# Seven block products instead of eight in the feed-forwards of a two-layer trunk

## The chip, the cores and the metric

The kernel runs on one core of a Trainium2 chip. The metric is device time in microseconds (us). The kernel before took 2554.37 us, the median of three runs (2552.99 to 2556.95). The engines are named as the profile names them: PE is TensorE's matmul side, PEld its weight loads, DVE is VectorE, ACT is ScalarE, POOL is GpSimd, SP is SyncE, whose queue issues the loads of weights.

## The reference, cut to what matters

Two layers act on 128 prompt tokens and 512 sample tokens (640 together, T), with 1024 features. Each layer has a gated feed-forward, a mixer, and a second feed-forward; the mixer of layer 0 is a convolution beside a recurrent scan, that of layer 1 is windowed attention. All is float32.

```python
def swiglu(h, w_in, w_out):
    gt, up = jnp.split(h @ w_in, 2, axis=-1)
    return (jax.nn.silu(gt) * up) @ w_out

def ffn_sublayer(x, mod, g, w_in, w_out, slot):
    h = pre_norm(x, g, mod[:, 3 * slot], mod[:, 3 * slot + 1])
    return x + 0.5 * mod[:, 3 * slot + 2] * swiglu(h, w_in, w_out)
```

`w_in` is 1024 x 5632 (2816 gate and 2816 value features), `w_out` is 2816 x 1024. `mod` is the modulation: `silu(cond) @ w_mod[l] + b_mod[l]`, nine slots of 1024 features per layer, for the two conditions (prompt and sample). There are four feed-forwards; below they are called FFN 1 to 4 (layer 0 first, layer 0 second, layer 1 first, layer 1 second).

## The kernel before, in words

Activations lie feature-major: a tile is 128 features by 640 tokens. A float32 product is made exact by splitting each operand into a high and a low part (`split_x`, L515: a cast on ACT gives the high part, a subtraction on DVE the low part) and summing three products on PE: high*high, high*low, low*high (`product_steps`, L523).

A feed-forward (`ffn`, L554) runs in parts of 8, 8 and 6 tiles of 128 hidden features (`PARTS`). For each hidden tile it loads a 1024 x 128 slice of the gate's weights (`raw_wg`) and one of the value's (`raw_wu`), splits both, and for two chunks of tokens (`CHUNKS`: 256 and 384 columns) sums 8 blocks x 3 terms into a PSUM bank for the gate (`pg`) and one for the value (`pu`). ACT applies silu to `pg`, DVE multiplies by `pu`, and the result `g` is split again. After a part, `project_out` (L591) sums the part's hidden tiles through `w_out` into `po`, and DVE adds the gated result to the residual x (L605).

The last tiles of `project_out` before a norm run chunk by chunk: the 256-column chunk of all of them, then the 384-column chunk. `norm_stats` (L434) makes the reciprocal root of the mean square and spreads it over all partitions (`nb`); `norm_apply` (L445) makes the normalized, modulated operand h, again as high and low part. So a next feed-forward's first products, on the first chunk, can run while the second chunk is normalized.

The modulation's weights (16 of 18 slots) are read during the feed-forwards as fillers: `mod_step` (L311) multiplies a 128 x 1024 slice `raw_wm` by the condition on DVE, four instructions of 512 elements, and sums over eight steps; `mod_sum` (L327) finishes a slot on PE. `plan` (L186) deals the fillers evenly over the hidden tiles and the tiles of `project_out`. The first two slots, which FFN 1 needs at once, run through PE instead (`mod_piece`, L290: 256 features, two loads of 512 KB, 16 matmul records and two transposes).

All weights come through one ring of six raw buffers of 512 KB on SP's queue (`load_w`, L470), issued ahead of their use; an issue waits until the ring's oldest buffer has been read. A framework orders the instructions of every engine from their priorities and from when it thinks their inputs ready; each engine then executes its own list strictly in order.

Of the kernel before, what the change touches and what calls it, by code (L numbers as in the profile page):

```python
# [16 lines left out]
P = 128  # L17
# [7 lines left out]
PARTS = ((0, 8), (8, 8), (16, 6))  # L25
# [10 lines left out]
EARLY, EARLY_TILES = 0, 2  # L36
# [24 lines left out]

def run(steps):
    for _ in steps:
        pass


class Trunk:
    def __init__(self, ctx, tc, i, o):
# [4 lines left out]
        self.rawp = pool("raw", 6)  # L73
        self.wp = pool("w", 3)
# [87 lines left out]
    def banks(self, n_mm, n_acc=0, n_mod=0):  # L162
        """the eight PSUM banks: for products, for sums held over several steps, for the modulation, for the rest"""
# [22 lines left out]
    def plan(self, n, points, skip):  # L186
        """the next n fillers go to the next so many points"""
        points -= skip
        self.points = [0] * skip + [-(-n * (p + 1) // points) + (-n * p // points) for p in range(points)]
# [60 lines left out]
    def transpose_x(self, rows):  # L250
        """x feature-major, and 1 / sqrt(mean square + eps) by token on all partitions"""
# [26 lines left out]
    def conditions(self):  # L278
        """conditions after silu, by feature"""
# [104 lines left out]
    def rstd(self, sq_tiles, blocks, scale_col, eps, name, eng=None):  # L384
        """1 / sqrt(mean + eps) by token, tokens on partitions: [P, len(blocks)]; tiles with their first tokens"""
# [16 lines left out]
    def inv_root(self, r, x, scale, name, eng=None):  # L402
        """r = scale / sqrt(x), x > 0: a guess from the exponent, a Newton step and one of third order (1e-9)"""
# [59 lines left out]
    def norm_chunk(self, n, c):  # L463
        self.norm_apply(n, c, self.norm_stats(n, c), range(KD))
# [22 lines left out]
    def split_w_slots(self, raw, name):  # L487
        """the same with the parts in slots, until free(name)"""
# [34 lines left out]
    def product_steps(self, ps, w, x, c0, n):  # L523
        """ps += w.T @ x, float32 operands as exact sums of two float32r parts"""
# [11 lines left out]
    def ffn_first(self, l, which, j):  # L536
        """the weights of a tile of hidden features, for the gate and for the value, with names"""
# [3 lines left out]
    def prefetch(self):  # L541
        """weights of the next phase's start, into slots"""
# [11 lines left out]
    def ffn(self, l, which, n, last):  # L554
        nc = self.nc
        w_out = self.i["ffn_w_out"][l, which]
        for part, (f0, fn) in enumerate(PARTS):
            ghi, glo = [], []
            def weights(j):
                return [(self.weights(*x), x[1]) for x in self.ffn_first(l, which, j)]  # L560

            def tile_chunk(j, w, c):
                (wg, gname), (wu, uname) = w
                c0, cw = CHUNKS[c]
                if c == 0:
# [20 lines left out]
            if part == 2:  # L586
                self.free_h()
# [848 lines left out]
```

## Time and profile before

| | |
|---|---|
| median of three runs | 2554.37 us (2552.99 to 2556.95) |
| profiled execution, span from first to last instruction | 2550.6 us |
| PE busy | 2503.3 us, 98% of the span |
| DVE busy | 1513.1 us, 59% |
| ACT busy | 815.9 us, 32% |
| POOL busy | 193.1 us, 8% |
| read from HBM | 248.3 MB, 99 GB/s over the span |

The page gives the profiled execution by its span alone; the median of the runs is 3.8 us above that span. Matmuls overlap in the records, so the duration of one (335 ns for 384 columns) is not what it costs; the distance from one start to the next is, and a run of many shows it best. The four feed-forwards fill 25.4 to 508 us, 869.5 to 1341.9 us, 1341.9 to 1806 us and 2081.1 to 2545 us of the span.

### The profile page before, as it was taken

Reading aid. Unit: us, or ns where it says so; the run is one execution under the profiler, and the core shown is the slowest. Engines: PE = TensorE matmul, PEld = TensorE weight load, DVE = VectorE, ACT = ScalarE, POOL = GpSimd, SP = SyncE. Lnnn points to the kernel's source line nnn. Section 1 sums busy time; section 2 is a strip of 40 time slices with the busy share of each in tenths; the row PEclk is TensorE's granted clock in tenths of the full one; section 3 lists DMA queues with packets and bytes.
Section 4 is the critical chain, followed back from the end, with each engine's and each line's share of the span. In section 5 each row is a group of like instructions: output and inputs, shape, how many; then the busy total and the mean of one; then the engine's idle time right before and its main releaser. Section 6 shows DMA issues by size and latency. Waiting matters only on the chain. (4 is left out here: it accounts for less than half of the span.)

```text
span 2550.6 us, 42680 instructions
## 1 busy us (share of the span) xinstructions
PE 2503.3 (98%) x17802; PEld 2440.3 (96%) x17802; DVE 1513.1 (59%) x2733; ACT 815.9 (32%) x1519; POOL 193.1 (8%) x282
## 2 busy tenths in 40 slices
PE   8999999999989999999999999999999999999999
PEld 5999999999989999999999999999988899999999
DVE  6765665569987766455556544545667863333333
ACT  5222212443234422221233212223465642222121
POOL 0000000124143000000010000000122010000000
PEclk9999999999999999999999999999999999999999
DMA  8654444311211344344433433433200122222221
GB/s 279 186 157 133 139 143 136 105 53 54 61 32 42 94 124 142 107 133 133 122 103 101 132 108 108 124 106 118 59 19 15 42 84 68 82 75 75 83 63 54
DMA packets 368522, 254.50 MB, mean 100 GB/s; under 512 B 8789, under 2 KB 350152, under 8 KB 368328
## 3 DMA queue, kind: packets, MB, share of 16 engines
q1 hardware_dynamic: 363384, 248.35, 32.3%
q10 hardware_dynamic: 4944, 3.41, 0.4%
q8 instruction: 140, 2.29, 0.4%
q14 instruction: 54, 0.44, 0.1%
HBM read 248.32 MB, written 3.41 MB: 99 GB/s over the span
## 5 line engine op out<-in xcount | busy, mean ns | idle before, releaser
L531 PE MATMUL po<-g,whi_o 128*128 128x256 f32 (+1 forms) x2672 | 573.4, 307 | 0.0
L531 PE MATMUL pg<-h,whi_wg 128*128 128x256 f32 (+1 forms) x2656 | 572.5, 307 | 0.0
L531 PE MATMUL pu<-h,whi_wu 128*128 128x256 f32 (+1 forms) x2656 | 568.2, 306 | 0.3 <-DVE nt L456 0.3
L531 PEld LDWEIGHTS po<-g,whi_o 128*128 128x128 f32 x2672 | 442.7, 188 | 3.7 <-ACT whi_o L517 1.2
L531 PEld LDWEIGHTS pg<-h,whi_wg 128*128 128x128 f32 x2656 | 441.3, 188 | 2.9 <-issue 2.5
L531 PEld LDWEIGHTS pu<-h,whi_wu 128*128 128x128 f32 x2656 | 439.9, 188 | 0.6 <-issue 0.6
L325 DVE SCALAR_TENSOR_TENSOR ma<-raw_wm,cond,ma 128x512 f32<-128x512 f32 x448 | 316.6, 747 | 205.2 <-DMA raw_wm<-in_w_mod 205.1
L531 PE MATMUL po<-g,wlo_o 128*128 128x256 f32 (+1 forms) x1336 | 408.5, 306 | 0.0
L531 PE MATMUL pg<-h,wlo_wg 128*128 128x256 f32 (+1 forms) x1328 | 406.8, 306 | 0.0
L531 PE MATMUL pu<-h,wlo_wu 128*128 128x256 f32 (+1 forms) x1328 | 405.8, 306 | 0.0
L605 DVE SCALAR_TENSOR_TENSOR x<-po,modG,x 128x256 f32<-128x256 f32 (+1 forms) x384 | 156.5, 435 | 240.3 <-PE po L531 239.3
L531 PEld LDWEIGHTS po<-g,wlo_o 128*128 128x128 f32 x1336 | 250.8, 188 | 0.0
L531 PEld LDWEIGHTS pg<-h,wlo_wg 128*128 128x128 f32 x1328 | 250.2, 188 | 0.0
L531 PEld LDWEIGHTS pu<-h,wlo_wu 128*128 128x128 f32 x1328 | 249.3, 188 | 0.0
L517 ACT CAST whi_o<-raw_o 128x1024 fp32r<-128x1024 f32 (+3 forms) x113 | 104.4, 924 | 385.7 <-PE po L531 246.2
L575 DVE TENSOR_TENSOR sil<-sil,pu 128x256 f32<-128x256 f32 (+1 forms) x176 | 85.3, 485 | 204.5 <-PE pu L531 200.7
L517 ACT CAST g<-sil 128x256 fp32r<-128x256 f32 (+1 forms) x176 | 80.4, 457 | 307.7 <-DVE sil L575 307.6
L518 DVE TENSOR_TENSOR wlo_wu<-raw_wu,whi_wu 128x1024 fp32r<-128x1024 f32 x83 | 101.5, 1223 | 119.3 <-ACT whi_wu L517 119.3
L517 ACT CAST whi_wg<-raw_wg 128x1024 fp32r<-128x1024 f32 x83 | 87.3, 1051 | 255.4 <-issue 130.7
L517 ACT CAST whi_wu<-raw_wu 128x1024 fp32r<-128x1024 f32 x83 | 87.2, 1050 | 216.8 <-PE pg L531 167.0
L382 POOL TENSOR_TENSOR acc<-acc,sq 128x256 f32<-128x256 f32 (+1 forms) x44 | 41.9, 954 | 1442.7 <-ACT sq L381 1442.5
L518 DVE TENSOR_TENSOR wlo_o<-raw_o,whi_o 128x1024 fp32r<-128x1024 f32 (+3 forms) x113 | 121.5, 1075 | 30.7 <-ACT whi_o L517 28.6
(412 smaller groups left out, 3470.5 us busy)
## 6 DMA issues: line engine op xcount, KB each, us to landing
raw_wm<-in_w_mod SPq DMA_DIRECT2D x144, 512.0 KB, 3.6
raw_wg<-in_ffn_w_in SPq DMA_DIRECT2D x88, 512.0 KB, 3.8
raw_wu<-in_ffn_w_in SPq DMA_DIRECT2D x88, 512.0 KB, 4.0
raw_o<-in_ffn_w_out SPq DMA_DIRECT2D x64, 512.0 KB, 4.1
raw_o<-in_ffn_w_out SPq DMA_DIRECT2D x32, 384.0 KB, 3.5
raw_z<-in_ev_w_in SPq DMA_DIRECT2D x8, 512.0 KB, 3.8
raw_oq<-in_od_w_in SPq DMA_DIRECT2D x8, 512.0 KB, 3.7
raw_o<-in_od_w_out SPq DMA_DIRECT2D x16, 256.0 KB, 2.7
```

The costliest lines, as they stand in the source:

```text
L325: nc.vector.scalar_tensor_tensor(out=acc, in0=part, scalar=col, in1=acc, op0=ALU.mult, op1=ALU.add)
L382: nc.gpsimd.tensor_tensor(out=self.acc[:, c0:c0 + n], in0=self.acc[:, c0:c0 + n], in1=sq[:, 0:n], op=ALU.add)
L517: nc.scalar.copy(out=hi, in_=src)
L518: nc.vector.tensor_tensor(out=lo, in0=src, in1=hi.bitcast(F32), op=ALU.subtract)
L531: self.last_mm = nc.tensor.matmul(ps, lhsT=a[k], rhs=b[k][:, c0:c0 + n], start=(k == 0 and j == 0), stop=(k == nk - 1 and j == 2))
L575: nc.vector.tensor_tensor(out=s, in0=s, in1=pu, op=ALU.mult)
L605: nc.vector.scalar_tensor_tensor(out=xs, in0=ps[:, s0 - c0:s0 - c0 + sn], scalar=self.modG[:, n, m, g:g + 1], in1=xs, op0=ALU.mult, op1=AL ...
```

## The change

Gate and value weights of a hidden tile are taken as a 2 x 2 block matrix: A11 and A12 are the gate's halves over the first and second 512 input features, A21 and A22 the value's. The operand h is a 2 x 2 block matrix too: halves of the features by halves of the tokens (320 and 320, `HALVES`). The eight block products become seven on sums of blocks (Winograd's form of Strassen's scheme): products 1 to 7 on A11, A12, S4, A22, S1, S2, S3 against B11, B21, B22, T4, T1, T2, T3. Four sums of weights (S1 to S4) per hidden tile are made on DVE, the sums of operands (T1 to T4) once per feed-forward on DVE and POOL. Three banks (`pb`) hold products 1, 6, 7 and 4 of three tiles, two (`pc`) products 5 and 3, one (`pa`) product 2; between products ACT copies the partial sum to SBUF (`st`) and DVE adds.

Besides: parts are 6, 6, 6 and 4 tiles; the ring of raw buffers has four entries instead of six, the split weights six of one kind instead of three and three; three of the filler slots become `mod_piece` calls, four in each of FFN 1 to 3, so 13 filler slots stay (5, 4, 4); fillers go 0.4 shares to a hidden tile and 1 to a tile of `project_out`; a feed-forward's first weights are no longer split ahead into slots; `project_out` ahead of a feed-forward uses the halves.

```diff
-PARTS = ((0, 8), (8, 8), (16, 6))
+HALVES = ((320, 320), (0, 320))
+HW = 320
+PARTS = ((0, 6), (6, 6), (12, 6), (18, 4))
...
+START_PAIRS = 3
+IN_SHARE = 0.4
+POST_AHEAD = 200
...
-        self.rawp = pool("raw", 6)
-        self.wp = pool("w", 3)
+        self.rawp = pool("raw", 4)
+        self.wp = pool("w", 6)
+        self.stp = pool("st", 6)
...
+    def norm_pair(self, n, c, pb, q):
...
+        for k, col in ((q, (0, 1)[c]), (q + 4, (3, 2)[c])):
+            for s0, sn, g in segments(t0, w):
+                a = slice(s0 - t0, s0 - t0 + sn)
+                nc.vector.scalar_tensor_tensor(out=f[:, col, a], in0=self.X[k][:, s0:s0 + sn],
+                                               scalar=self.modA[:, n, k, g:g + 1], in1=pb[:, a],
+                                               op0=ALU.mult, op1=ALU.mult)
+                nc.scalar.activation(out=f[:, col, a], in_=f[:, col, a], func=AF.Identity, bias=shift[:, k, g:g + 1])
...
+        if c == 0:
+            self.B["11", q], self.B["21", q] = parts("bc", f[:, 0:4:3])
+            return
+        flat = self.full[q]
+        t = self.slot(f"t13_{q}"), self.slot(f"t24_{q}")
+        nc.vector.tensor_tensor(out=t[0], in0=flat[:, HW:3 * HW], in1=flat[:, 0:2 * HW], op=ALU.subtract)
+        nc.gpsimd.tensor_tensor(out=t[1][:, 0:HW], in0=t[0][:, HW:], in1=f[:, 0], op=ALU.add)
+        nc.gpsimd.tensor_tensor(out=t[1][:, HW:], in0=f[:, 3], in1=t[1][:, 0:HW], op=ALU.subtract)
...
+        self.split_x(f[:, 2], *self.B["22", q])
+        self.B["T2", q], self.B["T4", q] = parts("td", view(t[1]))
...
+                first = js[:START_PAIRS]
+                jobs += [(j, i) for j in first for i in (1, 2)]
+                jobs += [(first[0], i) for i in (5, 6, 3, 7)]
...
+            jobs += [(j, i) for j in js for i in (1, 5, 6, 2, 7, 3, 4)]
...
+    def strassen(self, p, j, i, bank, g):
...
+            if i == 5:
+                src = summed("S1", a21, a22, ALU.add)
+            elif i == 6:
+                src = summed("S2", p["S1"], a11, ALU.subtract)
+            elif i == 7:
+                src = summed("S3", a11, a21, ALU.subtract)
+            elif i == 3:
+                src = summed("S4", a12, p["S2"], ALU.subtract)
...
+            w = self.wp.tile([P, KD * P], F32R, tag="w", name=f"ws{i}_{j}").rearrange("p (k m) -> p k m", m=P)
+            self.split_x(src, w[:, 0:4], w[:, 4:8])
...
+        for k in range(4):
+            xhi, xlo = self.B[x, k]
+            for t, (a, b) in enumerate(((w[:, k], xhi), (w[:, k], xlo), (w[:, 4 + k], xhi))):
+                nc.tensor.matmul(ps, lhsT=a, rhs=b, start=(i in (1, 5, 2) and k == 0 and t == 0),
+                                 stop=(k == 3 and t == 2), skip_group_check=True)
+        with self.tc.high_priority(offset=POST_AHEAD):
+            if i in (1, 5, 6):
+                p[i] = t = self.stp.tile([P, HW], F32, tag="st", name=f"st{i}")
+                nc.scalar.copy(out=t, in_=ps)
+            elif i == 4:
+                nc.vector.tensor_tensor(out=p[1], in0=p[1], in1=ps, op=ALU.mult)
+                self.hidden(g, j, 0, p[1])
+            else:
+                t = p[{2: 1, 7: 5, 3: 6}[i]]
+                nc.vector.tensor_tensor(out=t, in0=t, in1=ps, op=ALU.add)
+                if i != 7:
+                    nc.scalar.activation(out=t, in_=t, func=AF.Silu)
...
+        pieces = [((0, 0), (0, 2)), ((0, 1), (0, 8)), ((1, 0), (1, 2))]
```

Three places show how the order moves. First, DVE's list in the middle of a part of FFN 1, about hidden tile 8 (`wlo_w...`: low parts of split weights, `ma`: the fillers' sums; in the new rows `ws<i>_<j>` is the split weight of product i of tile j, S1 a buffer that holds one of the four weight sums, `st` the partial results). Before:

```order
L518 TENSOR_TENSOR wlo_wg00_9_2275<-raw_wg00_9_2272,whi_wg00_9_2274 128x1024
L325 SCALAR_TENSOR_TENSOR ma5_0_0_2395<-raw_wm0_5_2_2672,cond_100,ma5_0_0_2395 128x512
L575 TENSOR_TENSOR sil_2200<-sil_2200,pu_2151 128x256
L325 SCALAR_TENSOR_TENSOR ma5_0_1_2396<-raw_wm0_5_2_2672,cond_100,ma5_0_1_2396 128x512
L518 TENSOR_TENSOR g8_2149<-sil_2200,g8_2149 128x256
L325 SCALAR_TENSOR_TENSOR ma5_1_0_2397<-raw_wm0_5_2_2672,cond_100,ma5_1_0_2397 128x512
L325 SCALAR_TENSOR_TENSOR ma5_1_1_2398<-raw_wm0_5_2_2672,cond_100,ma5_1_1_2398 128x512
L518 TENSOR_TENSOR wlo_wu00_9_2281<-raw_wu00_9_2278,whi_wu00_9_2280 128x1024
```

The same place now, on the same engine:

```order
L746 TENSOR_TENSOR st1_2036<-st1_2036,pa_2081 128x320
L704 TENSOR_TENSOR S1_8_2175<-raw_wg00_8_2153,raw_wu00_8_2173 128x512
L602 TENSOR_TENSOR ws6_8_2196<-S1_8_2175,ws6_8_2196 128x512
L349 SCALAR_TENSOR_TENSOR ma3_1_0_1711<-raw_wm0_3_5_2288,cond_103,ma3_1_0_1711 128x512
L746 TENSOR_TENSOR st5_2058<-st5_2058,pb_2023 128x320
L602 TENSOR_TENSOR ws2_8_2213<-raw_wg00_8_2153,ws2_8_2213 128x512
L746 TENSOR_TENSOR st6_2076<-st6_2076,pc_2045 128x320
L602 TENSOR_TENSOR ws7_8_2232<-S1_8_2175,ws7_8_2232 128x512
L750 TENSOR_TENSOR st6_2076<-st6_2076,st5_2058 128x320
L704 TENSOR_TENSOR S1_8_2175<-raw_wg00_8_2153,S1_8_2175 128x512
L602 TENSOR_TENSOR g7_2132<-st6_2076,g7_2132 128x320
L742 TENSOR_TENSOR st1_2036<-st1_2036,pb_2023 128x320
```

Where the list held six instructions per hidden tile and the fillers, it now holds eighteen, and three additions of a PSUM bank per tile stand between the weights of the next tile.

Second, DVE's list at the start of FFN 3, in the norm of the second chunk of tokens (`nb3_1` is the spread reciprocal root, `nt` and `h` the operand before; `hf` the normalized operand, `tc`, `td`, `bd` parts of the block sums now). Before:

```order
L460 SCALAR_TENSOR_TENSOR h7_13223<-nt_13316,modv1_103,h7_13223 128x128
L460 SCALAR_TENSOR_TENSOR h7_13223<-nt_13316,modv1_103,h7_13223 128x256
L575 TENSOR_TENSOR sil_13374<-sil_13374,pu_13325 128x256
L325 SCALAR_TENSOR_TENSOR ma5_1_0_13682<-raw_wm1_5_1_13813,cond_100,ma5_1_0_13682 128x512
L518 TENSOR_TENSOR g0_13323<-sil_13374,g0_13323 128x256
```

The end of that norm now, and what follows it:

```order
L534 TENSOR_TENSOR t13_3_14017<-hf3_13896 128x640
L602 TENSOR_TENSOR bd3_14025<-hf3_13896,bd3_14025 128x320
L602 TENSOR_TENSOR tchi3_14022<-t13_3_14017,tchi3_14022 128x640
L602 TENSOR_TENSOR tdlo3_14028<-t24_3_14018,bd3_14025 128x640
L746 TENSOR_TENSOR st1_14049<-st1_14049,pa_14054 128x320
L704 TENSOR_TENSOR S1_0_14147<-raw_wu10_0_14145 128x512
L704 TENSOR_TENSOR S2_0_14167<-S1_0_14147,raw_wg10_0_14031 128x512
L746 TENSOR_TENSOR st1_14087<-st1_14087,pa_14092 128x320
```

The whole norm of the second half, 32 instructions from the spread root on, now stands ahead of the first addition that empties the bank `pa`, and ahead of the first weight sum S1.

Third, PE's list at the same place, from the matmul that spreads the root. Before:

```order
L432 MATMUL nb3_1_13263<-ident_79,r_n3_1_13260 128x128 x3
L531 MATMUL pu_13325<-h2_13176,wu10_0_0_12727 128x256 x2
L531 MATMUL pu_13325<-h2_13176,wu10_0_1_12728 128x256
L531 MATMUL pu_13325<-h3_13181,wu10_0_0_12727 128x256 x2
L531 MATMUL pu_13325<-h3_13181,wu10_0_1_12728 128x256
```

And now:

```order
L457 MATMUL nb3_1_13937<-ident_82,r_n3_1_13934 128x128 x2
L459 MATMUL nb3_1_13937<-ident_82,r_n3_1_13934 128x64
L735 MATMUL pb_14036<-bclo3_13902,ws1_0_14033 128x320
L735 MATMUL pb_14036<-bchi3_13901,ws1_0_14033 128x320
L735 MATMUL pb_14074<-bclo3_13902,ws1_1_14071 128x320
L735 MATMUL pb_14074<-bchi3_13901,ws1_1_14071 128x320
L735 MATMUL pb_14112<-bchi3_13901,ws1_2_14109 128x320
L735 MATMUL pb_14112<-bclo3_13902,ws1_2_14109 128x320
```

Behind these come the twelve matmuls of product 2 of tile 0 (bank `pa_14054`), then product 2 of tile 1, whose `pa_14092` is the same bank. Before, PE went on with the first chunk and then mixed in the second chunk feature by feature (`h0`, `h1`, ...); now seven left-over matmuls and one product are all that stands ahead of the reuse of `pa`.

## Rows read from the trace of the kernel before

**Rows 1.** The page, busy time by engine (share of span, instructions).

```profile
PE 2503.3 (98%) x17802; PEld 2440.3 (96%) x17802; DVE 1513.1 (59%) x2733; ACT 815.9 (32%) x1519; POOL 193.1 (8%) x282
```

**Rows 2.** Chain that ended last, in FFN 4: start us, us, what, matmuls.

```profile
2113.34 2.72 PE pg L531 x24
...
2118.78 4.16 PE pg L531 x24
...
2195.89 55.04 PE po L531 x384
```

**Rows 3.** Busy time by engine, window 208.5:378.1: PE, PEld, DVE, ACT, POOL, clock, DMA.

```profile
208.50:378.10 169.60, 169.60 (x1208) 166.97 (x1207) 106.19 (x172) 39.23 (x60) 0.00 (x0) 1.00 0.46 142
```

**Rows 4.** Groups of DVE instructions by shape: count, busy us, mean ns, idle before.

```profile
L325 DVE SCALAR_TENSOR_TENSOR ma<-raw_wm,cond,ma 128x512 f32<-128x512 f32 x448 | 316.6, 747 | 205.2 <-DMA raw_wm<-in_w_mod 205.1
...
L456 DVE SCALAR_TENSOR_TENSOR nt<-x,modA,nb 128x256 f32<-128x256 f32 x96 | 43.8, 475 | 5.3 <-PE nb L432 2.6 <-POOL acc L382 2.5
...
L518 DVE TENSOR_TENSOR wlo_o<-raw_o,whi_o 128x768 fp32r<-128x768 f32 x34 | 33.6, 987 | 10.8 <-ACT whi_o L517 10.1
...
L323 DVE TENSOR_SCALAR ma<-raw_wm,cond 128x512 f32<-128x512 f32 x64 | 28.6, 481 | 32.7 <-DMA raw_wm<-in_w_mod 32.4 <-PE pg L531 0.3
...
L456 DVE SCALAR_TENSOR_TENSOR nt<-x,modA,nb 128x128 f32<-128x128 f32 x48 | 16.4, 343 | 3.8 <-PE nb L432 3.8
...
L518 DVE TENSOR_TENSOR wlo_o<-raw_o,whi_o 128x512 fp32r<-128x512 f32 x13 | 8.9, 682 | 2.1 <-ACT whi_o L517 1.8
...
L518 DVE TENSOR_TENSOR o<-raw_o,o 128x640 fp32r<-128x640 f32 x6 | 4.8, 820 | 0.3 <-ACT o L517 0.3
```

**Rows 5.** Line 924: duration ns min/median/max, first and last start, shape.

```profile
L924 DVE TENSOR_TENSOR qp<-qp,tt x48: 474/484/1073, 585.2 to 822.7; 128x320 f32<-128x320 f32 x48
```

**Rows 6.** DVE's instructions in order of time, 196 to 290 us: start, us, what.

```profile
202.10 2.08 DVE L325 SCALAR_TENSOR_TENSOR ma<-raw_wm,cond,ma 128x512 f32<-128x512 f32 x3 [4.01 <-DMA raw_wm<-in_w_mod]
```

**Rows 7.** The first window: 16 records of one modulation sum and two transposes on PE.

```profile
1454.20:1510.90 56.70, 1.51 (x18) 1.00 0.39 118
```

**Rows 8.** PE's instructions in order of time, 40 to 49 us.

```profile
40.92 0.64 PE L299 MATMUL mps<-raw_wm,cond 128*32 128x256 f32 x8
41.49 0.44 PE L531 MATMUL pg<-h,wg 128*128 128x384 f32 x1
...
42.11 0.43 PE L304 MATMUL mps<-ident,msb 128*128 128x128 f32 x2
42.30 0.60 PE L531 MATMUL pu<-h,wu 128*128 128x384 f32 x2
```

**Rows 9.** POOL and DVE in order of time, 588 to 592 us.

```profile
589.04 1.70 POOL L925 TENSOR_TENSOR k<-k,tt 128x320 f32<-128x320 f32 x2 [3.17 <-ACT km L909]
...
589.10 1.98 DVE L924 TENSOR_TENSOR qp<-qp,tt 128x320 f32<-128x320 f32 x2
```

**Rows 10.** Windows about an idle stretch of PE: columns of rows 3.

```profile
712.00:716.00 4.00, 0.27 (x2) 0.28 (x3) 4.00 (x5) 1.14 (x3) 3.92 (x5) 0.64 0.00 0
716.00:722.20 6.20, 6.20 (x39) 6.20 (x39) 5.69 (x7) 0.43 (x2) 3.61 (x6) 0.68 0.01 3
```

**Rows 11.** Windows of the first eight hidden tiles of FFN 2, 3, 4.

```profile
869.50:987.60 118.10, 117.64 (x808) 116.48 (x808) 76.84 (x140) 39.24 (x72) 0.00 (x0) 0.99 0.37 114
1341.90:1454.30 112.40, 112.40 (x789) 112.40 (x789) 67.00 (x121) 36.48 (x68) 0.00 (x0) 1.00 0.36 110
2081.10:2195.80 114.70, 114.70 (x794) 114.63 (x795) 44.45 (x84) 36.60 (x67) 0.00 (x0) 0.99 0.21 62
```

**Rows 12.** Windows at the start: first 30 us, first eight tiles of FFN 1.

```profile
0.00:30.00 30.00, 17.54 (x106) 11.62 (x107) 17.50 (x46) 19.71 (x47) 1.20 (x17) 0.89 0.99 305
...
25.40:152.00 126.60, 126.05 (x895) 115.67 (x896) 95.86 (x188) 41.22 (x79) 0.20 (x3) 0.98 0.66 204
```

**Rows 13.** Waits: engine, line, waited for, us in total, times, longest.

```profile
DVE ma L325 <- DMA raw_wm<-in_w_mod: 205.1, 87, 4.6
...
DVE ma L323 <- DMA raw_wm<-in_w_mod: 32.4, 12, 4.9
```

More of the change, by code (lines that the diff above doesn't have):

```diff
@@ L59, in segments, with cut, blocks @@
     return out
+def cut(n):
+    return CHUNKS if n % 3 == 1 else HALVES
+def blocks(c0, w):
+    return [min(t, c0 + w - P) for t in range(c0, c0 + w, P)]
 def run(steps):
@@ L184, in fill, with plan @@
                 self.fillers.pop(0)()
-    def plan(self, n, points, skip):
-        points -= skip
-        self.points = [0] * skip + [-(-n * (p + 1) // points) + (-n * p // points) for p in range(points)]
+    def plan(self, n, shares):
+        total, at, done = sum(shares), 0.0, 0
+        self.points = []
+        for share in shares:
+            at += share
+            upto = min(n, int(n * at / total + 0.999))
+            self.points.append(upto - done)
+            done = upto
     def point(self):
@@ L428, in inv_root, with spread @@
         add_times(r, u, 1.875 * scale, y)
-    def spread(self, col, out):
-        self.nc.tensor.transpose(out, col.to_broadcast([P, P]), self.ident)
+    def spread(self, col, out, first=0):
+        n = out.shape[1]
+        if n == P:
+            self.nc.tensor.transpose(out, col.to_broadcast([P, P]), self.ident)
+        else:
+            self.nc.tensor.matmul(out, lhsT=col.to_broadcast([P, P]), rhs=self.ident[:, first:first + n], start=True,
+                                  stop=True, skip_group_check=True)
     def norm_stats(self, n, c):
-        c0, w = CHUNKS[c]
-        blocks = list(range(c0, c0 + w, P))
-        r = self.rstd([(a, 0) for a in (self.acc, *self.accs)], blocks, self.ones_d, self.eps, f"n{n}_{c}")
+        c0, w = cut(n)[c]
+        starts = blocks(c0, w)
+        r = self.rstd([(a, 0) for a in (self.acc, *self.accs)], starts, self.ones_d, self.eps, f"n{n}_{c}")
         pb = self.mm(f"nb{n}_{c}")
-        for j, t0 in enumerate(blocks):
-            self.spread(r[:, j:j + 1], pb[:, t0 - c0:t0 - c0 + P])
+        done = c0
+        for j, t0 in enumerate(starts):
+            self.spread(r[:, j:j + 1], pb[:, done - c0:t0 + P - c0], done - t0)
+            done = t0 + P
         if c == 1:
@@ new lines, in ffn, with bank, do @@
+        w_out = self.i["ffn_w_out"][l, which]
+        pairs = {}
+        mm = self.bank["mm"]
+        ring = {"b": mm[0:3], "c": mm[3:5], "a": mm[5:6]}
+        g = {}
+        def bank(kind, name):
+            ring[kind].append(ring[kind].pop(0))
+            return self.psum.tile([P, 512], F32, tag=f"bank{ring[kind][-1]}", name=name)[:, 0:HW]
+        def do(j, i):
+            p = pairs.setdefault(j, dict(done=set()))
+            for r, nm in enumerate(("gate", "up")):
+                if nm not in p and (r == 0 or i not in (1, 2)):
+                    p[nm] = self.early.pop((j, nm), None)
+                    if p[nm] is None:
+                        p[nm] = self.load_w(*self.ffn_first(l, which, j)[r])
+            self.strassen(p, j, i, bank, g)
@@ new lines, in ffn @@
+        for at, (j, i) in enumerate(jobs):
+            do(j, i)
+            if i == 4:
+                self.point()
+                if (l, which, j) in self.pieces:
+                    self.mod_piece(*self.pieces.pop((l, which, j)))
+                    if not self.pieces:
+                        self.free("cond32")
+            if at + 1 in ends:
+                part = ends[at + 1]
+                f0, fn = PARTS[part]
+                if part == len(PARTS) - 1:
+                    self.free_operand()
+                js = range(f0, f0 + fn)
+                run(self.project_out(w_out[f0 * P:(f0 + fn) * P, :], [g[j][0] for j in js], [g[j][1] for j in js], n,
+                                     final=(part == len(PARTS) - 1), last=last))
+                self.free(*[f"g{j}" for j in js])
@@ L591, in project_out, with hidden @@
+    def hidden(self, g, j, c, s):
+        if j not in g:
+            g[j] = self.two(f"g{j}", F32R)
+        hi, lo = g[j]
+        t0 = HALVES[c][0]
+        self.split_x(s, hi[:, t0:t0 + HW], lo[:, t0:t0 + HW])
     def project_out(self, w, xhi, xlo, n, final, last=False):
@@ L1357, in run @@
                 self.fillers.append(lambda: (self.vec_block(2), self.even_constants(), self.odd_constants()))
[L1358 to L1360 removed]
+            self.plan(len(self.fillers), shares)
             if (l, which) == (0, 0):
```

153 lines of the change are left out of this document (93 added, 60 removed).

## The prediction

> **What bounds the kernel now.** I read the busy times first: TensorE (PE) is busy for 98% of the span, VectorE (DVE) for 59% [rows 1]. A busy PE says little of what a matmul costs, so the chain that ended last comes next. In FFN 4 it is nothing but PE, in runs of 24 matmuls: 2.72 us with 256 columns, 4.16 us with 384 [rows 2]. That is 113.3 and 173.3 ns from start to start, 0.443 and 0.451 ns a column. A hidden tile is two runs of each, 13.76 us; a tile of the output projection in a part of eight is 55.04/8 = 6.88 us [rows 2]. So feed-forwards are bound by PE's columns, and a column removed there counts until another engine is late. The windows say who that would be: in a part of FFN 1 with its output projection DVE is busy 106 of 170 us, ACT 39 [rows 3].
>
> **In-products.** A hidden tile has 16 blocks x 3 terms x 640 columns now, and 7 products x 4 blocks x 3 terms = 84 matmuls of 320 columns after. No row has 320 columns. The nearest, 256 and 384, bound one at 113 and 173 ns, that is 9.5 and 14.6 us a tile; their prices per column give 141.7 and 144.4 ns, and I take 144 because both rows agree on the column within 2%. A tile then takes 12.1 us, 1.66 less, and 88 tiles 146 us less.
>
> The Trainium skill (TensorE: Matmul & The Clock Gate, Back-to-back issue gap) gives N/2.4 + 2.5 ns for an isolated matmul, an estimate of 135.8 ns at 320 columns, by which the sum would be some 60 us further down. At 256 and 384 columns it gives 109.2 and 162.5 where the rows have 113.3 and 173.3, so the measurement decides against it.
>
> **Smaller things on PE.** In projections that change from 256 + 384 to 320 + 320 a pair costs 288 ns instead of 286.7; 1440 such pairs are +2 us. Twelve modulation pieces replace three sums. A sum costs 56.70 - 55.04 = 1.66 us [rows 2, 7]. A piece is two groups at 0.57 us and two transposes at 0.19 [rows 8], 1.33 us. Net 12 x 1.33 - 3 x 1.66 = +11 us. That there are four parts instead of three adds no matmul.
>
> **DVE, the cover that gets thin.** In a hidden tile the order shows eleven instructions of 512 elements (four weight sums, seven low parts) and seven of 320. Alone these take 682 and 484 ns [rows 4, 5]. Behind one another they overlap: three fillers take 2.08 us, not 3 x 0.747 [rows 4, 6], so 0.08 us less each. A tile is 11 x 0.60 + 7 x 0.40 = 9.5 us beside 12.1 on PE. An output tile of a six-tile part is 0.91 for the low part (987 ns alone) and 1.05 for three additions to x of 320, 128 and 192 columns, interpolated from 343 and 475 ns [rows 4]: 1.96 us beside 5.2. A filler step is 4 x 0.67 = 2.7 us. FFN 1 then asks 22 x 9.5 + 24 x 1.96 + 8 x 1.65 (four-tile part) + 5 slots x 20.3 + 22 for the norm = 392 us of DVE, against 22 x 12.1 + 152 + 14 (sums and pieces) = 432 on PE. FFN 2 and 3, with four slots, ask 371 against 430, FFN 4 290 against 418. So nothing is over in total, but the slack is 40 and 59 us where it was over a third of the time.
>
> Into that slack falls what DVE loses by its order. Its fillers waited 205.1 + 32.4 us for their loads, 1.85 us per step over 128 steps [rows 13]. Behind a waiting filler now stand the weight sums and the additions that empty PSUM (first place in the order): product 4 needs the addition of product 7, which has only product 3, 1.7 us, to happen in. The ring that feeds them shrinks to four buffers, two of which a hidden tile holds almost throughout. If lateness per step stays, FFN 1 loses 74 us and FFN 2 and 3 59 each; over the slack that is 34 us in all. If every instruction also took its time alone, 55 us more per feed-forward, it would be 193. If the split weights (six products deep, some 10 us of PE's work) absorb it all, it is 0. I take 30, near the first, because the overlap is what the rows show in a dense stretch.
>
> **Starts of the feed-forwards.** Here the cover is gone. Before, PE mixed the second chunk's products in feature by feature; now (second and third places) DVE has 32 instructions of the second half's norm ahead of the first addition that empties `pa`, and PE has 19 matmuls, 2.7 us, until it needs that bank. The 32 are 16 scalar-tensor-tensors of 128 and 192 columns (343 ns and, interpolated, 409), 4 of 320 and 12 of 640 (820 ns) [rows 4, 5]: 17.8 us alone, 15.3 overlapped. The last one waits for two POOL additions and a cast, +1.5; the addition itself is 0.4. So PE stands for 17.2 - 2.7 = 14.5 us. POOL's eight additions run at the same time: beside two of them, 1.70 us, two DVE instructions of 320 took 1.98 us instead of 0.89 [rows 9, 5]. All 6.8 us of POOL at that rate would cost 4.4; I take half, 2.2.
>
> The Trainium skill (GPSIMD Engine Reference, its table of specifications) says that GpSimd contends with VectorE's instructions that have two SBUF inputs. Half of the 32 read the spread root from PSUM. By that rule the loss stays at the half taken; without it, all of it.
>
> After an idle stretch PE's clock is down: 0.68 over the 6.2 us after the wait at 716 us [rows 10], half the time at its lower level, so 2 us are lost. With 1.5 for the norm's small matmuls the start of FFN 2 and of FFN 3 costs 20.2 us above 8 tiles at their rate. Before, it cost 118.1 - 110.1 = 8.0 and 112.4 - 110.1 = 2.3 [rows 11, 2]. That is +12 and +18. In FFN 4 the additions are mixed into the norm; PE has 55 matmuls, 7.9 us, against 20.4 of DVE including two sums and two low parts. 12.5 + 2.2 + 2 + 1.5 - 4.6 = +14. In FFN 1 PE's first product now stands behind six of eight modulation pieces, not two: 4 MB more at 305 GB/s, 13.8 us later [rows 12]; half of the norm (11 us) follows the last load. PE is at its rate from about 58 us with 10 us of products done, where it had been 16.5 us behind at 25.4 [rows 12]: +6, and +4 for DVE, which the three first tiles then occupy. I take +10, between 0 and 20. Together +54; without contention, and with the norm mixed in well, half.
>
> **Sum.** -146 + 2 + 11 + 54 + 30 = -49 us on a span of 2550.6, so 2501.6. The median of the runs lies 3.8 above the span: 2505.
>
> **Rivals.**
> - The waits are absorbed. Ring, split weights and order keep DVE ahead, and the starts cost half: -30 - 27, about 2448. For it: total slack of 40 to 59 us. Against it: the bank `pa` is single, and nothing else stands in PE's list. A matmul at 141.7 ns would add -24 more.
> - DVE sets the pace in FFN 1 to 3, slower than before. One mechanism: the filler's load is issued only when the four-deep ring frees a buffer, DVE waits for it in order, and the additions behind it hold PSUM. For it: 237 us of such waits while DVE had time to spare. Against it: a late DVE finds its loads landed. From 79 us of such loss, 26 per feed-forward, the gain is gone; at 110 us the time is 2585, at the bound of 193 it is 2668.
> - The gain is mostly eaten: starts at 20 us more (lone durations, full contention) and waits of 45: 2540.
> - A matmul of 320 runs at the rule's 135.8 ns: 10,000 of them at 8 less, 2425.
>
> **Numbers.** The measurement can tell 0.2%, 5 us. My forecast, 2475 to 2530, has 0.50. Absorbed waits 0.15, the faster matmul 0.03, the eaten gain 0.12 (0.07 still faster, 0.05 within 0.2%), DVE's pace 0.20. So faster 0.75, same 0.05, slower 0.20. For 8 in 10 the range goes from 2440 into the slower case as far as 2585.
>
> **What would show it.** Right: runs of 12 matmuls about 1.73 us apart in the middle of FFN 4, hidden tiles at 12.1; one idle stretch of PE of 12 to 17 us at the start of FFN 2, 3 and 4, ended by an addition from `pa` on DVE, with the clock low behind it; DVE above 85% busy in FFN 1 to 3, PE waiting there on DVE for few us. Wrong: hidden tiles of FFN 4, which has no fillers, well off 12.1 us (then the price per column failed); no long idle stretch at the starts; or PE waiting in FFN 1 to 3 on DVE additions behind fillers for more than 26 us each, which would make it slower.

## The result and the profile after

The changed kernel is slower: 2623.11 us median (2622.05 to 2629.03), 1.0274 times the kernel before (95% interval 1.0256 to 1.0292), where 2505 with a range of 2440 to 2585 had been forecast. The profiled execution has a span of 2621.3 us, 70.7 above the 2550.6 of before.

The page, busy time by engine, the line that answers to [rows 1], and the granted clock of TensorE in 40 slices of the span, in tenths:

```profile
PE 2466.8 (94%) x16976; PEld 2368.3 (90%) x16976; DVE 2021.0 (77%) x3816; ACT 1141.7 (44%) x2312; POOL 222.7 (8%) x308
...
PEclk7899999999999889999998899999999998999999
```

PE, 98% busy before, now has 154 us in which it does nothing, and its clock is down in four places: the beginning and slices 14 to 15, 22 to 23 and 34, where FFN 2, 3 and 4 begin. In the middle of FFN 4 nothing is wrong; the chain that ended last there (start us, us, what, matmuls), to be held against [rows 2]:

```profile
2300.19 1.76 PE pb L735 x12
2301.95 1.76 PE pc L735 x12
2303.71 1.76 PE pb L735 x12
```

Twelve matmuls take 1.76 us, 146.7 ns each, not 144; a hidden tile is 84 x 146.7 = 12.32 us instead of 13.76. Now the windows of each feed-forward's first part, six tiles from the first product to the first matmul of the output projection (start:end, us, then busy us of PE, PEld, DVE, ACT, POOL, clock, DMA share, GB/s). They answer to [rows 11, 12]:

```profile
38.10:151.50 113.40, 98.43 (x614) 85.00 (x615) 88.44 (x170) 54.33 (x112) 6.36 (x6) 0.86 0.42 125
893.60:1015.90 122.30, 94.56 (x618) 86.47 (x617) 87.96 (x171) 59.94 (x124) 9.42 (x8) 0.86 0.33 99
1383.10:1506.90 123.80, 93.96 (x602) 86.14 (x602) 87.50 (x169) 57.72 (x120) 9.43 (x8) 0.85 0.34 99
2158.60:2257.40 98.80, 79.25 (x530) 78.38 (x530) 76.82 (x142) 57.13 (x117) 9.39 (x8) 0.90 0.22 65
```

And the six tiles of the second part of FFN 2 and of FFN 3, with fillers beside them:

```profile
1061.20:1135.60 74.40, 74.02 (x504) 73.76 (x504) 65.36 (x117) 41.40 (x81) 0.00 (x0) 1.00 0.38 110
1552.30:1628.30 76.00, 74.80 (x506) 73.80 (x504) 64.73 (x117) 40.08 (x80) 0.00 (x0) 1.00 0.35 101
```

Six tiles are 73.9 us of matmuls. These two second parts take that and 0.5 and 2.1 us more; the first parts take it and 39.5, 48.4, 49.9 and 24.9 more, 162.7 together. Before, eight tiles of 110.1 us took 16.5, 8.0, 2.3 and 4.6 more, 31.4. The balance of the two spans:

| term | forecast | measured |
|---|---|---|
| hidden tiles, 88 x (12.32 - 13.76) | -146 | -126.7 |
| 1440 pairs of 320 + 320 in projections, 2 x 146.7 against 286.7 ns | +2 | +9.6 |
| first parts: 162.7 - 31.4; FFN 1's first product at 38.1 instead of 25.4 us | +54, and 16 for twelve pieces | +131.3 + 12.7 |
| all else (fillers, ends of parts, mixers) | +30, and -5 for three sums | +43.8, what is left over |
| sum | -49 | +70.7 |

The whole miss is 120 us; 74 of it lies in the first parts. By feed-forward, FFN 1 to 4, the first parts cost 36, 40, 48 and 20 us more than before, pieces included and in FFN 1 the late first product; 10, 12, 18 and 14 had been forecast, and 5.3 for the four pieces in each of FFN 1 to 3. FFN 3 shows how. DVE there, in order of time (start us, us, what; in brackets the idle time before and what ended it):

```profile
1389.70 0.18 DVE L422 RECIPROCAL r_n<-r_n 128x3 f32<-128x3 f32 x1 [1.82 <-ACT r_n L421]
1390.77 2.42 DVE L517 SCALAR_TENSOR_TENSOR hf<-x,modA,nb 128x128 f32<-128x128 f32 x8 [0.90 <-PE nb L459]
...
1397.73 0.82 DVE L602 TENSOR_TENSOR tdlo<-t,tdhi 128x640 fp32r<-128x640 f32 x1 [1.51 <-ACT tdhi L601]
...
1402.61 0.82 DVE L602 TENSOR_TENSOR tdlo<-t,bd 128x640 fp32r<-128x640 f32 x1 [1.25 <-ACT bd L601]
...
1407.47 0.82 DVE L602 TENSOR_TENSOR tdhi<-t,tdhi 128x640 fp32r<-128x640 f32 x1 [1.51 <-ACT tdhi L601]
1408.21 0.41 DVE L517 SCALAR_TENSOR_TENSOR hf<-x,modA,nb 128x192 f32<-128x192 f32 x1
...
1413.29 0.83 DVE L602 TENSOR_TENSOR tdlo<-t,bd 128x640 fp32r<-128x640 f32 x1 [1.51 <-ACT bd L601]
1414.04 0.48 DVE L746 TENSOR_TENSOR st<-st,pa 128x320 f32<-128x320 f32 x1
```

The norm's second half takes 23.3 us from its first instruction to the start of the addition that empties `pa`; 16.8 had been worked out (17.2 with the addition itself). DVE stands four times, 1.2 to 1.5 us each, for a cast that follows POOL's addition; the forecast had counted one such wait at the end. What PE waited for in the same part (engine, line, waited for, us in total, times, longest):

```profile
PE pa L735 <- DVE hf L517: 17.0, 1, 17.0
PE pc L735 <- ACT ws L601: 4.4, 1, 4.4
PE pa L735 <- DVE st L746: 2.7, 2, 2.3
PE pc L735 <- DVE ma L704: 2.6, 1, 2.6
PE mps L323 <- DMA raw_wm<-in_w_mod: 1.8, 2, 1.1
PE mps L328 <- ACT msb L326: 1.3, 2, 0.8
```

The first and third rows are PE's waits for the norm, 19.7 us; 14.5 had been forecast. Where they stand (PE, columns as for DVE):

```profile
1391.50 0.31 PE L735 MATMUL pb<-bchi,ws 128*128 128x320 f32 x1
1408.77 0.61 PE L735 MATMUL pa<-bchi,ws 128*128 128x320 f32 x1 [16.95 <-DVE hf L517]
...
1414.57 0.64 PE L735 MATMUL pa<-bchi,ws 128*128 128x320 f32 x1 [2.26 <-DVE st L746]
```

PE stops after the seven left-over matmuls, before product 2 of tile 0, and not after the 19 of the forecast. What releases it is not the addition from `pa` but the last `hf` at 1408.21, the 28th of the norm's 32 instructions. In the kernel, `ring["a"]` (L644) is the bank that was taken last, and that is the one from which `hf` still reads the spread root `nb`; so product 2 has no bank until the norm has read it. The addition ends only the second wait, 2.3 us. It stands behind all 32, so PE would have had to wait for it also with another bank for `nb`; no run tries that.

The second and fourth rows are new: weights of tiles 3 and 2 that come late. The last two are the pieces. And behind each wait the clock is down. Windows of PE, columns as above:

```profile
1391.00:1409.00 18.00, 1.04 (x7) 0.81 (x6) 12.97 (x28) 11.68 (x28) 7.05 (x6) 0.58 0.00 0
1409.00:1420.00 11.00, 8.30 (x34) 7.65 (x35) 6.67 (x11) 5.48 (x9) 2.38 (x2) 0.60 0.00 0
...
1440.00:1450.00 10.00, 7.00 (x34) 6.17 (x34) 5.78 (x13) 2.96 (x6) 0.00 (x0) 0.66 0.46 137
...
1460.00:1470.00 10.00, 4.78 (x29) 2.56 (x28) 6.16 (x13) 2.48 (x5) 0.00 (x0) 0.78 0.54 157
```

Taken from matmul start to matmul start, FFN 3's 49.9 us are 24.0 before products that waited, 8.1 in 74 matmuls at half rate (2 had been forecast), 14.9 in the four pieces with the waits inside and right behind them, the late weights among these (5.3), and 2.7 in the norm's small matmuls (1.5). The first window also has a DMA share of 0.00: no load is on its way while PE stands.

In FFN 4 the additions from `pa` are mixed into the norm, as the forecast had it, and PE waits once, for the split weights of product 5, whose sum S1 comes on DVE behind the norm; 12.5 to 14.7 us had been worked out there:

```profile
PE pc L735 <- ACT ws L601: 19.4, 1, 19.4
```

### The profile page after: what moved, and what is told of

The parts are those of the page before. It is cut to its first block, busy times and chain, and to the rows that moved or that the text cites. A ratio compares the mean times of both kernels' runs of the same rounds, so it can differ in the third digit from the quotient of the medians.

```text
span 2621.3 us, 43402 instructions
## 1 busy us (share of the span) xinstructions
PE 2466.8 (94%) x16976; PEld 2368.3 (90%) x16976; DVE 2021.0 (77%) x3816; ACT 1141.7 (44%) x2312; POOL 222.7 (8%) x308
## 5 line engine op out<-in xcount | busy, mean ns | idle before, releaser
L615 PE MATMUL po<-g,whi_o 128*128 128x320 f32 (+2 forms) x2672 | 593.8, 311 | 4.0 <-ACT g L601 2.8
L615 PEld LDWEIGHTS po<-g,whi_o 128*128 128x128 f32 x2672 | 446.6, 188 | 14.4 <-ACT g L601 4.0
L615 PE MATMUL po<-g,wlo_o 128*128 128x320 f32 (+2 forms) x1336 | 412.7, 310 | 0.0
L776 DVE SCALAR_TENSOR_TENSOR x<-po,modG,x 128x128 f32<-128x128 f32 (+3 forms) x480 | 196.7, 435 | 139.9 <-PE po L615 138.4
L601 ACT CAST ws<-S 128x512 fp32r<-128x512 f32 x303 | 188.2, 621 | 253.5 <-DVE S L704 61.9
L735 PE MATMUL pb<-tdhi,ws 128*128 128x320 f32 x1100 | 247.3, 312 | 9.4 <-DVE st L746 8.3
L602 DVE TENSOR_TENSOR ws<-S,ws 128x512 fp32r<-128x512 f32 x303 | 209.9, 694 | 57.3 <-ACT ws L601 56.9
L735 PE MATMUL pa<-bchi,ws 128*128 128x320 f32 x704 | 175.8, 318 | 37.1 <-DVE hf L517 31.4
L735 PEld LDWEIGHTS pb<-tdhi,ws 128*128 128x128 f32 x1100 | 184.8, 190 | 15.9 <-DVE st L746 12.0
L735 PE MATMUL pb<-tdlo,ws 128*128 128x320 f32 x616 | 191.0, 312 | 0.0
L735 PE MATMUL pb<-bchi,ws 128*128 128x320 f32 x704 | 173.3, 314 | 5.8 <-ACT ws L601 4.8
```

The costliest lines, as they stand in the source:

```text
L601: nc.scalar.copy(out=hi, in_=src)
L602: nc.vector.tensor_tensor(out=lo, in0=src, in1=hi.bitcast(F32), op=ALU.subtract)
L615: self.last_mm = nc.tensor.matmul(ps, lhsT=a[k], rhs=b[k][:, c0:c0 + n], start=(k == 0 and j == 0), stop=(k == nk - 1 and j == 2))
L735: nc.tensor.matmul(ps, lhsT=a, rhs=b, start=(i in (1, 5, 2) and k == 0 and t == 0), stop=(k == 3 and t == 2), skip_group_check=True)
L776: nc.vector.scalar_tensor_tensor(out=xs, in0=ps[:, s0 - c0:s0 - c0 + sn], scalar=self.modG[:, n, m, g:g + 1], in1=xs, op0=ALU.mult, op1=AL ...
```

## The experiments

Ratios are to the kernel before, with 95% intervals; "excess" is the time of a first part above its matmuls.

**The width by itself.** 96 matmuls of a width, one after the other, fp32r, on zeros.

> Nothing of the network is computed: 96 matmuls of each of several widths (256 to 512 columns and some below), fp32r operands, one bank each, on zeros. In the changed kernel a matmul of 320 columns came every 146.7 ns, where the prediction took 144 from rows of 256 (113.3) and 384 (173.3). If the price belongs to the width, 320 takes 146.7 here too and the widths between do not lie on one line (the line through 256 and 384 gives 143.3 at 320, 128.3 at 288, 158.3 at 352). If it comes from this kernel (banks that are emptied meanwhile, busy engines beside), 320 takes 143 to 144 here.

Seven of its windows, 192 and 128 columns last (start:end, us, PE busy, ..., clock before the last two columns); the widths are 256, 320, 384, 448, 512, 192, 128. The first holds 91 matmuls from start to start, the others 96:

```profile
28.93:39.85 10.92, 10.92 (x93) 10.92 (x92) 0.69 (x1) 0.00 (x0) 0.00 (x0) 1.00 0.00 0
...
77.76:91.83 14.07, 14.07 (x99) 14.07 (x97) 0.47 (x1) 0.00 (x0) 0.00 (x0) 1.00 0.00 0
...
137.91:154.55 16.64, 16.64 (x97) 16.64 (x97) 0.54 (x1) 0.00 (x0) 0.00 (x0) 1.00 0.00 0
154.55:174.38 19.83, 19.83 (x97) 18.02 (x97) 0.56 (x1) 0.00 (x0) 0.00 (x0) 1.00 0.00 1
174.38:196.19 21.81, 21.81 (x97) 18.02 (x96) 0.62 (x1) 0.00 (x0) 0.00 (x0) 1.00 0.00 1
196.19:206.89 10.70, 10.70 (x98) 10.70 (x96) 0.69 (x1) 0.00 (x0) 0.00 (x0) 1.00 0.01 2
206.89:217.58 10.69, 10.69 (x98) 10.69 (x97) 0.36 (x1) 0.00 (x0) 0.00 (x0) 1.00 0.00 0
```

320 columns take 14.07/96 = 146.6 ns with nothing beside them, 384 take 173.3, both as in the kernels; 256 take 10.92/91 = 120.0, where the kernel before has 113.3. The price at 320 belongs to the width, and the line from 120.0 at 256 to 173.3 at 384 passes through it and, within 2 ns, through 288 (131.7) and 352 (160.0). What lay off the line is the row of 256 that the forecast went by.

**Without the pieces.** The three gates are left out and stand at zero.

```diff
-        self.pieces = {(*at, j): (*what, j) for at, what in pieces for j in range(4)}
+        self.pieces = {}
```

> The changed kernel without its twelve modulation pieces (three gates of the feed-forwards are left out and stand at zero). By their price on PE alone, 12 x 1.33 us, it is 16 us faster than the changed kernel, 2607. Start theory (the loss sits in the first part of each feed-forward, where pieces, late weights and a cold clock add up): FFN 3's first part loses 15 to 18 us of its 49.9 above its matmuls, FFN 1 and 2 as much, 45 to 55 us in all, about 2573. Rival (the ring of four buffers starves DVE throughout): 24 loads less, but the middle parts give back nothing beyond the 16 us.

2571.04 us (1.0070, 1.0055 to 1.0085), 52 less. Excess in FFN 1 to 3: 23.7, 33.1, 30.7, so 16, 15 and 19 less; FFN 4, which has no pieces, 25.8 instead of 24.9. At 1.33 us a piece only 16 of the 52 are PE's own work on them.

**Without the sums of blocks of the input.** In `norm_pair`:

```diff
-        nc.vector.tensor_tensor(out=t[0], ...); nc.gpsimd.tensor_tensor(...) x2
-        self.B["T1", q], self.B["T3", q] = parts("tc", view(t[0]))
+        self.B["T1", q], self.B["T3", q] = self.B["11", q], self.B["21", q]
-        self.B["T2", q], self.B["T4", q] = parts("td", view(t[1]))
+        self.B["T2", q], self.B["T4", q] = self.B["11", q], self.B["21", q]
```

> The changed kernel without the sums of blocks of the normed input: products 3 to 7 read the plain blocks instead (all matmuls stay), so the second half of each norm has 20 instructions on DVE instead of 32 and none on POOL. Start theory: DVE's 12 x 0.75 us and four waits of 1.5 us for POOL go, PE's idle stretch at FFN 2 and 3 falls from 17.3 to 3 to 6 us and the slow clock behind it from 8 to about 4; with FFN 4 and half as much in FFN 1 the time falls by 45 to 60 us, to about 2570. Rival (the addition that empties pa is stuck behind whatever DVE has there, and the weights are late anyway): 10 to 20 us.

2554.41 us (1.0007, 0.9997 to 1.0018), 69 less, more than expected. In FFN 4 the excess falls from 24.9 to 6.4, in FFN 3 from 49.9 to 27.1. PE's waits in FFN 3's first part:

```profile
PE pc L730 <- ACT ws L596: 7.4, 2, 4.5
PE mps L328 <- ACT msb L326: 0.9, 1, 0.9
PE mps L323 <- DMA raw_wm<-in_w_mod: 0.8, 1, 0.8
```

The 17.0 us for DVE's norm are gone; the late weights are still there. The edit does more than save the sums' time on DVE and POOL: products 4 to 7 now need only the first half of the tokens, and PE's list has product 5 of tile 0 ahead of product 2. So 69 us is the price of the sums together with what had to wait for them.

**Both left out.** The two edits above together.

> Both cuts in the changed kernel at once: without the sums of blocks of the normed input (products 3 to 7 read the plain blocks) and without the twelve modulation pieces. If the two costs stand one behind the other on PE's path, they add: 2623 - 52 - 69 = 2502, and the first parts of FFN 2 to 4 are left with 5 to 12 us each above their matmuls. If they overlap (the weights are late behind either), 2515 to 2540.

2504.09 us (0.9803, 0.9788 to 0.9817): 119 less, where 52 and 69 make 121. The costs add; neither hides the other. The excess is 17.8, 14.3, 11.0 and 8.0.

**The pieces elsewhere.** Those of FFN 2 and 3 at tiles 6 to 9 of the feed-forward before.

```diff
-        pieces = [((0, 0), (0, 2)), ((0, 1), (0, 8)), ((1, 0), (1, 2))]
+        pieces = [((0, 0), 0, (0, 2)), ((0, 0), 6, (0, 8)), ((0, 1), 6, (1, 2))]
```

> The changed kernel with the same twelve pieces, those of FFN 2 and FFN 3 moved into the second part of the feed-forward before each (tiles 6 to 9). Start theory: the first parts of FFN 2 and 3 lose 12 to 18 us each, the second parts of FFN 1 and 2 gain their plain price of 5.3 us each: 15 to 25 us faster, about 2600. Rival (a piece costs the same wherever it stands, because its loads go through the starved ring): no change within 5 us, or slower since fillers run there.

2607.41 us (1.0206, 1.0190 to 1.0222). Excess in FFN 2 and 3: 31.5 and 32.6, 17 less each; the second parts that took the pieces in are 7.8 and 8.9 us longer, more than 5.3. In a first part four pieces cost 17, in a second part 8 to 9.

**A ring of five.** Raw weights in five buffers, one pair of slots fewer.

```diff
-        self.rawp = pool("raw", 4)
+        self.rawp = pool("raw", 5)
```

> The changed kernel with five buffers instead of four for raw weights (paid for with one pair of slots fewer). If it is the ring that makes the weights late behind the pieces (34 of the 50 us that they cost are not their own work on PE), one buffer more gives back 10 to 25 us, all in the first parts of FFN 1 to 3: about 2605. If the lateness comes from what PE and DVE do in order (a piece's matmuls wait for their load with the next tile's products behind them), no change within 5 us.

2568.75 us (1.0063, 1.0039 to 1.0088), 54 less, more than twice the 10 to 25 that had been expected and as much as without pieces. Excess 23.5, 36.5, 35.4, 24.4: nothing changes in FFN 4. PE's waits in FFN 3's first part keep the norm and lose the weights:

```profile
PE pa L735 <- DVE hf L517: 17.0, 1, 17.0
PE pa L735 <- DVE st L746: 2.6, 2, 2.3
PE pc L735 <- ACT ws L601: 0.9, 1, 0.9
```

The reason is in the queue that issues loads. In the changed kernel (start us, us from the first issue of a group to the end of the last, what, count):

```profile
1353.02 3.29 SPq L559 DMA_DIRECT2D raw_wg<-in_ffn_w_in  x3
1358.44 63.12 SPq L559 DMA_DIRECT2D raw_wu<-in_ffn_w_in  x2
...
1428.29 7.81 SPq L559 DMA_DIRECT2D raw_wm<-in_w_mod  x3
1437.70 0.37 SPq L559 DMA_DIRECT2D raw_wu<-in_ffn_w_in  x1
```

And with five buffers, where FFN 3 begins 35.4 us earlier:

```profile
1311.84 4.68 SPq L559 DMA_DIRECT2D raw_wg<-in_ffn_w_in  x3
1318.06 3.89 SPq L559 DMA_DIRECT2D raw_wu<-in_ffn_w_in  x2
1384.71 0.34 SPq L559 DMA_DIRECT2D raw_wm<-in_w_mod  x1
```

Products 1 and 2 of three tiles stand ahead, so three gate weights lie in the ring until their tiles' sums S3 and S4 are made; with the value weight of tile 0 the four buffers are full for the whole norm. The second of the two value weights is issued 63 us after the first, when DVE has got to the sums, and the third only at 1437.70, behind a piece's loads; that of tile 3 follows at 1460.41, behind the next piece's. S1 of each waits for that, and from tile 2 on PE with it. With five buffers the second value weight is in 60 us before it is needed.

A full ring alone does not cost that. In FFN 4, which has neither pieces nor fillers, the three value weights take 69.8 us to be issued, and PE waits for nothing after its one wait of 19.4:

```profile
2132.42 69.76 SPq L559 DMA_DIRECT2D raw_wu<-in_ffn_w_in  x3
```

**Two tiles ahead instead of three.** The ring has four buffers again.

```diff
-START_PAIRS = 3
+START_PAIRS = 2
```

> The changed kernel with products 1 and 2 of two tiles ahead of the norm's end instead of three, all else as it is (ring of four). If the ring is short because the raw gate weights of three tiles lie in it until their last product, so that one buffer is left for value weights and pieces, a buffer more is free and the first parts of FFN 1 to 3 give back 8 to 15 us each, 25 to 45 in all: about 2590. Rival (the products ahead are what covers the norm): PE waits 3.5 us longer at each of four starts, 10 to 15 us slower, about 2635.

2595.29 us (1.0168, 1.0151 to 1.0185), 28 less: the excess is 32.7, 39.6, 37.6 and, in FFN 4, 27.8, 3 more. Holding one raw weight less is worth 7 to 12 us in each of FFN 1 to 3, though it takes cover away.

**POOL's additions on DVE.** In `norm_pair`:

```diff
-        nc.gpsimd.tensor_tensor(out=t[1][:, 0:HW], ...)
-        nc.gpsimd.tensor_tensor(out=t[1][:, HW:], ...)
+        nc.vector.tensor_tensor(out=t[1][:, 0:HW], ...)
+        nc.vector.tensor_tensor(out=t[1][:, HW:], ...)
```

> The changed kernel with the eight additions of 320 columns of the norm's second half on DVE instead of POOL. If POOL's handover and its contention with DVE cost what the trace shows (four idle times of 1.5 us on DVE before a low part, 1.70 us of POOL for two additions that DVE does in 0.8), the idle stretch of PE at the starts falls by 3 to 5 us in FFN 2 to 4: 10 to 15 us faster, about 2610. Rival (DVE is simply full there, and 8 x 0.4 us more on it outweigh the handovers): no change or up to 10 us slower.

2608.19 us (1.0206, 1.0191 to 1.0221), 15 less. PE's long wait in FFN 3 is 14.4 us instead of 17.0, with eight instructions more on DVE.

**Three repairs together.** The edits of the ring of five, of the moved pieces and of the additions on DVE.

> The changed kernel with three repairs at once: a ring of five, the pieces of FFN 2 and 3 moved into the second part of the feed-forward before, the norm's additions on DVE. Each alone gave 54, 16 and 15 us. If the moved pieces and the fifth buffer mend the same lateness, the sum is less than 85: 2623 - 54 - 15 - 5 = 2550, level with the kernel before; if they are independent, 2538. Above 2565 the third buffer reader (fillers in the middle) would be short as well.

2557.20 us (1.0011, 1.0002 to 1.0021), 66 less, not 85, and 7 above the expected level: the fifth buffer and the moved pieces mend the same lateness. The excess is 24.5, 23.5, 21.8, 20.8, still 59 us more than before the change.

**Sums of blocks beside plain tiles.** In the kernel before, parts of 6, 4, 4, 4, 4 tiles in FFN 1 and 4, 5, 5, 4, 4 in the others; the first part plain, the others as seven products; ring of four.

```diff
+            f = self.slot(f"f{k}")
+            nc.vector.tensor_tensor(out=f, in0=self.hhi[k].bitcast(F32), in1=self.hlo[k].bitcast(F32), op=ALU.add)
...
+                    if 0 <= q < 4:
+                        self.block_sums(q)
...
+                    for i in (1, 5, 6, 2, 7, 3, 4):
+                        self.strassen(p, j, i, bank, g)
```

> The kernel before with seven block products only from the second part of each feed-forward on: the first part (6 tiles in FFN 1, 4 in the others) stays plain and DVE makes the sums of blocks beside it, from the parts of the normed input; parts of 4 or 5 tiles behind it; one modulation slot as four pieces in FFN 1's first part, the others as fillers. Start theory: the starts cost what they cost before, and 16 + 3 x 18 tiles at 12.32 us instead of 13.76 save 101 us; pieces, shorter parts and lateness take back 15 to 35: 2470 to 2490. Rival (the seven products starve DVE wherever fillers run): the later parts of FFN 1 to 3 lie 10 us or more above their matmuls each, and the time is 2520 or more.

2508.72 us (0.9820, 0.9806 to 0.9835): 47 us faster than the kernel before, and the fastest here that leaves nothing out. It differs from the changed kernel in more than that: four pieces instead of twelve, shorter parts, 18 tiles left plain, all sums of blocks on DVE; no run takes these apart. FFN 3's plain part, then its first part of seven products:

```profile
1335.70:1395.00 59.30, 59.30 (x410) 59.20 (x410) 54.55 (x112) 26.34 (x51) 0.00 (x0) 1.00 0.22 67
...
1422.50:1485.40 62.90, 62.90 (x440) 62.13 (x439) 53.14 (x100) 33.82 (x68) 0.00 (x0) 1.00 0.38 109
```

Four plain tiles are 55.0 us and five others 61.6: 4.3 and 1.3 above. DVE is busy 92% of the plain part and PE does not wait. The time is 19 us above the top of the expected range (2470 to 2490): FFN 1's first part, with the initial pieces, four more and fillers, lies 24.7 above its matmuls (16.5 before), and the four ends of the last output projections 5 to 10 us each.

**The plain part one tile shorter.** In FFN 2 to 4:

```diff
-    ((0, 4), (4, 5), (9, 5), (14, 4), (18, 4))
+    ((0, 3), (3, 5), (8, 5), (13, 5), (18, 4))
```

> The version with a plain first part (2508.7), that part shortened from four to three tiles in FFN 2 to 4 (parts of 3, 5, 5, 5, 4). Three more tiles at 1.44 us less are 4 us: 2504. If DVE no longer finishes the sums of blocks inside three plain tiles and their output products (20 us of sums beside 41 + 21 us), PE waits at the second part and it is 5 us or more slower.

2531.68 us (0.9914, 0.9899 to 0.9929), 23 slower than four tiles, and not for the reason expected. PE's waits from 1394 to 1430 us, at the end of FFN 3's first output projection, and DVE's sums at the same place:

```profile
PE pc L687 <- ACT ws L526: 5.9, 1, 5.9
PE po L540 <- ACT whi_o L526: 1.5, 2, 0.9
```

```profile
1422.32 0.69 DVE L656 TENSOR_TENSOR S<-raw_wu 128x512 f32<-128x512 f32 x1 [0.64 <-DMA raw_wu<-in_ffn_w_in]
```

The first S1 waits for its value weight, issued only at 1417.52, and not for the sums of the input, the last of which DVE has finished at 1400.1. In FFN 2 PE stands 8 us at the same place, 4.1 of them for weights of the output projection and 3.2 for a modulation sum whose fillers are late. These are 14 of the 23 us; where the rest goes stays open.

## Why the prediction was wrong

**In-products (right in kind, 19 us too much).** The step "their prices per column give 141.7 and 144.4 ns" took 320 columns to cost like its neighbours. It takes 146.7. The price is not proportional to the columns: from 320 to 384 each adds 0.417 ns, on a constant of 13.3, so the price per column at 384 is too low for 320. And 256 columns in the kernel before had only half that constant (113.3 - 106.7), though by themselves they have all of it (120.0), so a line through the two rows is too low as well.

**Starts (the step that failed).** The forecast put +54 there and 16 for the pieces; 144 were measured. It named the right place and the right cause of the first wait, DVE's norm with the clock low behind it, but not the way it comes about: the long stretch at FFN 2 and 3 (14.5 and 17.0 us) is ended by the norm's reads of `nb` in the bank of `pa`, and in FFN 4 by the weights of product 5 (19.4); an addition from `pa` ends none of the three. That two of the three lie inside the 12 to 17 us of the forecast is in part luck, for in FFN 2 and 3 the wait at the addition, 2.5 and 2.3 us, comes on top. Without the sums of blocks and what waits for them 69 us go, so that term existed and was too small: 16.8 us of DVE up to the addition, 19.0 with what was set for POOL beside it, were 23.3, of which 4.3 are three more waits for POOL and a cast; and 2 us for the clock were 8 in FFN 3, where PE stands three times for long and not once.

What was missing altogether is the ring. "1.33 us a piece, net +11" priced the pieces by PE alone. The forecast did say that a ring of four is short, but as a loss of DVE on fillers in the middle. There it costs little: the later hidden tiles of FFN 1 to 3 lie 15.7 us above their matmuls in all, against 10.9 before. It is short at the start, where three gate weights are held for products ahead and the pieces' loads and the value weights queue behind them; one buffer more gives 54 us, one weight less held gives 28, and neither gains anything in FFN 4, which has neither pieces nor fillers.

**DVE on fillers (about right in size, for no reason that was tested).** 30 were set, and 43.8 remain for everything outside the first parts with three sums less; some 32 of these lie in the output projections (53 us above their matmuls, 22 before), which now take most fillers and end one part more. The rival "DVE sets the pace in FFN 1 to 3, slower" gave 2585 to 2668 and so holds the measured time, but not by its mechanism: DVE is 77% busy, and of the time in the four feed-forwards in which PE does nothing 92 us lie in the first parts and 18 outside them. Its sentence that the load waits until the ring frees a buffer was right; the place was not.

**The chances.** 0.20 for slower was too low. 14.5 us of stall, the clock and the pieces had been added as if each stood alone with a full queue of weights behind it.

## What to carry to other kernels

Fewer matmuls only pay where the operands they need are made beside other matmuls: here the seven products lose 69 us when PE waits for the sums and the pieces' loads, and win 47 when four to six plain tiles cover the sums and eight of the twelve pieces are fillers again. When products are put ahead to hide a wait, count which input buffers they hold and what cannot be loaded meanwhile: the wait comes back as late weights. Price a matmul of a new width by a run of that width, not by the columns of its neighbours.

## What the runs showed of the hardware

At a granted clock of 1.00 (2.4 GHz), fp32r matmuls behind one another, each with a weight load, took 120.0 ns at 256 columns, 146.6 at 320, 173.3 at 384 and 227.2 at 512, each within 1 ns of columns/2.4 plus 13.3; 304 took 137.8, 2.2 below that, and 448 took 206.6, 6.6 above. 192 and 128 columns took 111.4 both, so the 64 fewer saved nothing. In the kernel before, 256 columns took 113.3; what makes that difference was not tried. The Trainium skill (TensorE: Matmul & The Clock Gate, Back-to-back issue gap) has columns/2.4 plus 2.5 ns for an isolated matmul; no width here came that low, and the measurement decides.
